# Regrouping the rows of a store-bound top-2 gate kernel: 65 and 63 rows to 64 and 64, and fewer first loads

## The chip, the cores and the metric

The kernel runs on one core of one Trainium2 chip. The metric is the device time of the program in microseconds; for the kernel before it is the median of three runs. A profile of one execution gives a span, the time from the first to the last instruction that the profiler recorded, which is about 2 us shorter than the device time.

## The reference: what is computed

There are 16 x 1024 = 16384 tokens. Each has a row of 512 float32 values in `x` and 8 router logits. The two largest of the 8 softmax probabilities, scaled so that they add up to 1, each multiply the token's row, and both products are written, the smaller weight first.

```python
probs = np.exp(router_logits - logits_max)
probs = probs / np.sum(probs, axis=-1, keepdims=True)
topk_indices = np.argsort(probs, axis=-1)[..., -k:]            # k = 2
topk_probs = np.take_along_axis(probs, topk_indices, axis=-1)
topk_probs = topk_probs / np.sum(topk_probs, axis=-1, keepdims=True)
x_expanded = x[:, :, np.newaxis, :].repeat(k, axis=2)
return (x_expanded * topk_probs[..., np.newaxis]).astype(np.float32)
```

So 33.5 MB of `x` and 0.5 MB of logits are read, and 67.1 MB are written. After the scaling the two weights depend only on the difference of the two largest logits, and the kernel computes them as two sigmoids of it.

## The kernel before

The 16384 tokens are 128 per partition. They are worked on in two groups, of 65 and 63 tokens ("rows") per partition. In a group, partition p holds consecutive tokens, so a load of n rows reads n x 2 KB in one piece for each partition, and a store of n rows writes n x 4 KB in one piece.

The tile `xs` holds a whole group of `x`; `osp` is an output buffer of 16 rows. Half of the output doesn't go through `osp`: a multiply writes its output over rows of `xs`, its own input among them. `over(r, n, G)` gives the place: twice the row number, less G, so that the output of the group's last rows ends with the group's last row.

```python
GROUPS = [65, 63]
LOADS = [[2, 2, 4, 8, 17, 28, 4], [16, 16, 31]]
LAST = [[(48, 9), (57, 8)], [(48, 15)]]

...  # the top-2 weights: 11 small VectorE operations and 2 ScalarE sigmoids, giving WA

    L = 16
    logits = wpool.tile([P, M, E], F32)
    xs = wpool.tile([P, max(GROUPS), D], F32)
    osp = wpool.tile([P, L, 2, D], F32)

    def over(r, n, G):
        a = 2 * r - G
        return xs[:, a : a + 2 * n, :].rearrange("p (r k) d -> p r k d", k=2)

    h = L // 2
    e = 2
    m0 = 0
    for g, G in enumerate(GROUPS):
        r = 0
        for n in LOADS[g]:
            nc.sync.dma_start(xs[:, r : r + n, :], x_v[g][:, r : r + n, :])
            r += n
            if g == 0 and r == L:
                nc.sync.dma_start(logits[:, :G], rl_v[0])
                nc.sync.dma_start(logits[:, G:], rl_v[1])
                WA = top2_weights(nc, wpool, logits, M, E)
        assert r == G
        begin = [(0, e, osp[:, :e]), (e, L - e, osp[:, e:])] if g == 0 else [(0, L, osp)]
        plan = begin + [
            (L, L, over(L, L, 2 * L)),      # output over xs[0:32]
            (2 * L, h, osp[:, :h]),
            (2 * L + h, h, osp[:, h:]),
        ]
        plan += [(r, n, over(r, n, G)) for r, n in LAST[g]]
        for r, n, og in plan:
            nc.vector.tensor_tensor(og, ...xs rows r to r + n, WA..., op=ALU.mult)
            queue = nc.scalar if n == e else nc.sync
            queue.dma_start(o_v[g][:, r : r + n], og)
        m0 += G
```

The stores of group 0 therefore have 2, 14, 16, 8, 8, 9 and 8 rows, those of group 1 have 16, 16, 8, 8 and 15. All loads and all stores but one are issued in this order from one queue, SyncE's. What a transfer or a multiply must wait for (a load before the multiply that reads it, a store before the rows it reads are overwritten) the framework puts in.

Of the kernel before, what the change touches and what calls it, by code (L numbers as in the profile page):

```python
# [1 line left out]

# [4 lines left out]

F32 = mybir.dt.float32
ALU = mybir.AluOpType
ACTF = mybir.ActivationFunctionType  # L10
P = 128


def top2_weights(nc, pool, logits, M, E):

    hi, lo, n = None, None, E  # L20
    while n > 1:
        n //= 2
        if hi is None:
            a, b = logits[:, :, 0:n], logits[:, :, n : 2 * n]
            nhi = pool.tile([P, M, n], F32, tag=f"hi{n}")
            nlo = b
            nc.vector.tensor_tensor(nhi, a, b, op=ALU.max)  # L27
            nc.vector.tensor_tensor(nlo, a, b, op=ALU.min)  # L28
        else:
            a, b = hi[:, :, 0:n], hi[:, :, n : 2 * n]  # L30
            nhi = pool.tile([P, M, n], F32, tag=f"hi{n}")
            nlo = pool.tile([P, M, n], F32, tag=f"lo{n}")
            tmp = pool.tile([P, M, n], F32, tag=f"tmp{n}")
            nc.vector.tensor_tensor(tmp, lo[:, :, 0:n], lo[:, :, n : 2 * n], op=ALU.max)  # L34
            nc.vector.tensor_tensor(nlo, a, b, op=ALU.min)  # L35
            nc.vector.tensor_tensor(nlo, nlo, tmp, op=ALU.max)  # L36
            nc.vector.tensor_tensor(nhi, a, b, op=ALU.max)  # L37
        hi, lo = nhi, nlo
    dlt = pool.tile([P, M], F32, tag="dlt")
    nc.vector.tensor_tensor(dlt, hi[:, :, 0], lo[:, :, 0], op=ALU.subtract)  # L40
    WA = pool.tile([P, M, 2], F32, tag="WA")
    nc.scalar.activation(WA[:, :, 0], dlt, ACTF.Sigmoid, scale=-1.0)  # L42
    nc.scalar.activation(WA[:, :, 1], dlt, ACTF.Sigmoid, scale=1.0)  # L43
    return WA

GROUPS = [65, 63]

LOADS = [[2, 2, 4, 8, 17, 28, 4], [16, 16, 31]]


LAST = [[(48, 9), (57, 8)], [(48, 15)]]


@with_exitstack
def kernel(
    ctx: ExitStack,
    tc: tile.TileContext,  # L60
    x: bass.AP,
    router_logits: bass.AP,
    k: bass.AP,
    out: bass.AP,
):
    nc = tc.nc
    B, S, D = x.shape
    E = router_logits.shape[-1]
    N = B * S
    assert int(k) == 2 and E == 8 and N == P * sum(GROUPS)  # L70
    M = N // P

    L = 16
    x_v, o_v, rl_v = [], [], []
    t0 = 0
    for n in GROUPS:
        t1 = t0 + P * n
        x_v.append(
            x.rearrange("b s d -> (b s) d")[t0:t1].rearrange("(p m) d -> p m d", p=P)
        )  # L80
        o_v.append(
            out.rearrange("b s k d -> (b s) k d")[t0:t1].rearrange(
                "(p m) k d -> p m k d", p=P
            )
        )
        rl_v.append(
            router_logits.rearrange("b s e -> (b s) e")[t0:t1].rearrange(
                "(p m) e -> p m e", p=P
            )
        )  # L90
        t0 = t1

    wpool = ctx.enter_context(tc.tile_pool(name="wpool", bufs=1))
# [28 lines that stand above are left out]
            (L, L, over(L, L, 2 * L)),  # L122
            (2 * L, h, osp[:, :h]),
            (2 * L + h, h, osp[:, h:]),
        ]
        plan += [(r, n, over(r, n, G)) for r, n in LAST[g]]
        for r, n, og in plan:
            nc.vector.tensor_tensor(  # L128
                og,
                xs[:, r : r + n, :].unsqueeze(2).to_broadcast([P, n, 2, D]),  # L130
                WA[:, m0 + r : m0 + r + n, :].unsqueeze(3).to_broadcast([P, n, 2, D]),
                op=ALU.mult,
# [7 lines that stand above are left out]
# [1 line left out]
_INS = ['x', 'router_logits', 'k']  # L141
_OUTS = [((16, 1024, 2, 512), 'float32')]

_NUMBERS = {'k': 2}


# [26 lines left out]
```

## Time and profile before

| | |
|---|---|
| time, median of 3 runs | 240.35 us (240.12 to 240.47) |
| span of the profiled execution | 238.4 us |
| VectorE busy | 142.0 us in 23 instructions, 138.2 of it in the 12 multiplies of line 128 |
| ScalarE busy | 1.8 us in 3 instructions |
| read from HBM, written to it | 34.08 MB, 67.11 MB |
| mean rate over the span | 424 GB/s |
| DMA issues | 10 loads of x, 2 of logits, 12 stores |

How to read it: the page cuts the span into 40 slices (6 us each) and prints the busy share of each engine in tenths; the row "DMA" is the mean of the core's 16 DMA engines. A packet is the piece that one DMA engine moves for one partition; "landing" is the moment at which a transfer has told its semaphore that all of it has arrived, so the time from issue to landing contains the time in the queue. The chain of waits follows the work that ended last back from the end. A group's line gives the operation, its shape, how often it ran, its busy time and mean duration, and after the bar the idle time of the engine before it and what ended most of that.

### The profile page before, as it was taken

How to read it: one execution, taken by the hardware profiler on the slowest of the kernel's cores; microseconds unless marked ns; L12 is line 12 of the kernel's file. 1: busy time of each engine (PE TensorE's matmuls, PEld its weight loads, DVE VectorE, ACT ScalarE, POOL GpSimd, SP SyncE). 2: the span in 40 equal slices, each digit the busy share in tenths (PEclk: the TensorE clock that was granted, in tenths of full speed). 3: DMA queues.
4: the chain of work that ended last, by engine and by line, in shares of the span. 5: the costliest groups of instructions: out<-in, count | busy, mean ns of one | idle time of the engine just before them, and what ended most of it. 6: DMA issues, size and time to landing. Idle time of an engine off the chain costs nothing.

```text
span 238.4 us, 118 instructions
## 1 busy us (share of the span) xinstructions
DVE 142.0 (60%) x23; ACT 1.8 (1%) x3; POOL 0.2 (0%) x4
## 2 busy tenths in 40 slices
DVE  0058999990299699900000699999006999990000
ACT  2000000000000000000000000000000000000000
POOL 0000000000000000000000000000000000000000
DMA  7999989999898999999999999999998989999995
GB/s 247 443 470 389 496 359 521 352 462 462 352 506 352 440 440 440 440 408 472 440 434 418 418 484 426 426 440 429 407 473 352 528 352 440 440 440 429 495 402 258
DMA packets 3456, 101.19 MB, mean 425 GB/s; under 512 B 384, under 2 KB 512, under 8 KB 896
## 3 DMA queue, kind: packets, MB, share of 16 engines
q1 hardware_dynamic: 3312, 100.14, 97.9%
q10 hardware_dynamic: 144, 1.05, 1.0%
HBM read 34.08 MB, written 67.11 MB: 424 GB/s over the span
## 4 chain that ended last, share of the span: by engine, by line
DMA 43%; DVE 41%; issue 5%; SPq 1%; ACT 0%; DVEq 0%
DVE xs L128 22%; DVE osp L128 17%; DMA xs<-in_x_dram 13%; DMA out_dram<-osp 13%; DMA out_dram<-xs 12%; DMA logits<-in_router_logits_dram 5%; SPq L112 1%; DVE nhi L27 0%; DVE logits L28 0%; SPq L116 0%; DVE nlo L36 0%; DVE tmp L34 0%; DVE nhi L37 0%; DVE nlo L35 0%; SPq L136 0%
## 5 line engine op out<-in xcount | busy, mean ns | idle before, releaser
L128 DVE TENSOR_TENSOR osp<-xs,WA 128x8192 f32<-128x8192 f32 (+3 forms) x7 | 69.1, 9908 | 55.5 <-DMA xs<-in_x_dram 31.1
L128 DVE TENSOR_TENSOR xs<-xs,WA 128x16384 f32<-128x16384 f32 (+3 forms) x5 | 69.1, 13811 | 2.2 <-DMA out_dram<-xs 2.1
L27 DVE TENSOR_TENSOR nhi<-logits 128x512 f32<-128x512 f32 x1 | 0.7, 693 | 14.6 <-DMA logits<-in_router_logits_dram 14.6
L42 ACT ACT_TABLE_LOAD x1 | 1.3, 1283 | 0.7 <-PEq L154 0.7
L28 DVE TENSOR_TENSOR logits<-logits 128x512 f32<-128x512 f32 x1 | 0.7, 691 | 0.0
L36 DVE TENSOR_TENSOR nlo<-nlo,tmp 128x256 f32<-128x256 f32 (+1 forms) x2 | 0.7, 350 | 0.0
L37 DVE TENSOR_TENSOR nhi<-nhi 128x256 f32<-128x256 f32 (+1 forms) x2 | 0.7, 350 | 0.0
L35 DVE TENSOR_TENSOR nlo<-nhi 128x256 f32<-128x256 f32 (+1 forms) x2 | 0.7, 349 | 0.0
L42 ACT ACTIVATE WA<-dlt 128x128 f32<-128x128 f32 x1 | 0.3, 314 | 16.5 <-DVE dlt L40 16.5
L34 DVE TENSOR_TENSOR tmp<-logits 128x256 f32<-128x256 f32 x1 | 0.4, 417 | 0.0
L40 DVE TENSOR_TENSOR dlt<-nhi,nlo 128x128 f32<-128x128 f32 x1 | 0.3, 292 | 0.0
L43 ACT ACTIVATE WA<-dlt 128x128 f32<-128x128 f32 x1 | 0.3, 298 | 0.0
L34 DVE TENSOR_TENSOR tmp<-nlo 128x128 f32<-128x128 f32 x1 | 0.3, 284 | 0.0
L154 POOL MEMSET const-bfloat16-1.0<- 128x1 bf16 x1 | 0.1, 101 | 0.0
L154 POOL MEMSET const-uint8-127<- 128x1 uint8 x1 | 0.1, 101 | 0.0
L154 POOL MEMSET const-float32-0.0<- 128x1 f32 x1 | 0.1, 98 | 0.2 <-issue 0.2
L154 POOL MEMSET const-float32-1.0<- 128x1 f32 x1 | 0.1, 98 | 0.0
## 6 DMA issues: line engine op xcount, KB each, us to landing
out_dram<-osp SPq DMA_DIRECT2D x4, 4096.0 KB, 20.7
xs<-in_x_dram SPq DMA_DIRECT2D x2, 4096.0 KB, 29.9
xs<-in_x_dram SPq DMA_DIRECT2D x1, 7936.0 KB, 37.9
out_dram<-xs SPq DMA_DIRECT2D x1, 7680.0 KB, 23.2
xs<-in_x_dram SPq DMA_DIRECT2D x1, 7168.0 KB, 39.7
out_dram<-osp SPq DMA_DIRECT2D x1, 7168.0 KB, 27.5
out_dram<-xs SPq DMA_DIRECT2D x1, 4608.0 KB, 20.3
xs<-in_x_dram SPq DMA_DIRECT2D x1, 4352.0 KB, 21.2
```

Source lines behind the costliest of these rows:

```text
L27: nc.vector.tensor_tensor(nhi, a, b, op=ALU.max)
L28: nc.vector.tensor_tensor(nlo, a, b, op=ALU.min)
L34: nc.vector.tensor_tensor(tmp, lo[:, :, 0:n], lo[:, :, n : 2 * n], op=ALU.max)
L35: nc.vector.tensor_tensor(nlo, a, b, op=ALU.min)
L36: nc.vector.tensor_tensor(nlo, nlo, tmp, op=ALU.max)
L37: nc.vector.tensor_tensor(nhi, a, b, op=ALU.max)
L40: nc.vector.tensor_tensor(dlt, hi[:, :, 0], lo[:, :, 0], op=ALU.subtract)
L42: nc.scalar.activation(WA[:, :, 0], dlt, ACTF.Sigmoid, scale=-1.0)
L43: nc.scalar.activation(WA[:, :, 1], dlt, ACTF.Sigmoid, scale=1.0)
L112: nc.sync.dma_start(xs[:, r : r + n, :], x_v[g][:, r : r + n, :])
L128: nc.vector.tensor_tensor(og, xs[:, r : r + n, :].unsqueeze(2).to_broadcast([P, n, 2, D]), WA[:, m0 + r : m0 + r + n, :].unsqueeze(3).to_b ...
L154: nc = _bacc.Bacc("TRN2", target_bir_lowering=False, num_devices=1)
```

## The change

Both groups get 64 rows. The last multiply and store of each group take 16 rows (64 KB in one piece for each partition in the store) in place of 9 and 8 in group 0 and 15 in group 1; the list `LAST` goes. The 16 rows before the logits come in two loads, of 2 and 14 rows (4 and 28 KB), in place of 2, 2, 4 and 8, and the 17-row load (34 KB) becomes one of 16. It is meant to make the schedule regular and its transfers fewer and longer.

```diff
+GROUPS = [64, 64]
 
-GROUPS = [65, 63]
+LOADS = [[2, 14, 16, 28, 4], [16, 16, 32]]
 
-LOADS = [[2, 2, 4, 8, 17, 28, 4], [16, 16, 31]]
-
-
-LAST = [[(48, 9), (57, 8)], [(48, 15)]]
@@
             (L, L, over(L, L, 2 * L)),
             (2 * L, h, osp[:, :h]),
             (2 * L + h, h, osp[:, h:]),
+            (3 * L, L, over(3 * L, L, G)),
         ]
-        plan += [(r, n, over(r, n, G)) for r, n in LAST[g]]
```

With 64 rows the last output of a group lies over `xs[32:64]`. A partition's rows then begin every 128 KiB in `x` and every 256 KiB in the output, where they began every 130 and 260 KiB in group 0 and every 126 and 252 KiB in group 1.

## The prediction

> **What bounds the kernel now.** I read the 40-slice picture first, because a kernel that moves 101 MB and does one multiply per output element is a transfer kernel until shown otherwise.
>
> ```profile
> DVE  0058999990299699900000699999006999990000
> ...
> DMA  7999989999898999999999999999998989999995
> ...
> DMA packets 3456, 101.19 MB, mean 425 GB/s; under 512 B 384, under 2 KB 512, under 8 KB 896
> ...
> q1 hardware_dynamic: 3312, 100.14, 97.9%
> q10 hardware_dynamic: 144, 1.05, 1.0%
> ```
>
> The DMA row is 8 or 9 in every slice but the first and the last; VectorE has whole runs of zeros. The two queues add up to 98.9% of 16 engines' span. So what sets the end is the number of bytes, the rate of the 16 DMA engines, the time until the first byte and the time after the last. VectorE (142 us of 238.4) only has to hand over each store before the queue in front of it is empty.
>
> The chain of waits seems to say something else: it names VectorE for 39% of the span, in several places. It must be read with that picture:
>
> ```profile
> 150.18 30.59 DMA out_dram<-osp
> ...
> 180.87 0.10 DVE osp L128
> 180.96 8.51 issue
> 189.47 8.70 DVE osp L128
> 198.17 0.02 issue
> 198.19 16.16 DVE xs L128
> ```
>
> A 16-row store issued at 150.18 lands 30.6 us later although its data need about 19 us: the rest is queue. While VectorE makes the last three stores (180.87 to 214.35), the engines work off earlier ones. Whether that holds at the end is in the landing times (start of the issue, plus the us to landing in the table of DMA issues, asked in small windows). Group 1's stores land at 180.8 (150.18 + 30.6), 200.1 (167.44 + 32.7), 209.8 (189.6 + 20.2), 219.5 (198.2 + 21.3) and 237.6 (214.38 + 23.2). The gaps, 19.3, 9.7, 9.7 and 18.1 us, are for 8.39, 4.19, 4.19 and 7.86 MB: 432 to 434 GB/s each time, so no hole lies between them. The last store was issued 5.1 us before its predecessor landed: that is the slack of the tail.
>
> The VectorE waits, in the groups kept apart by shape, say which transfers gate it:
>
> ```profile
> L128 DVE TENSOR_TENSOR osp<-xs,WA 128x8192 f32<-128x8192 f32 x4 | 34.6, 8688 | 23.8 <-DMA out_dram<-osp 23.8
> L128 DVE TENSOR_TENSOR osp<-xs,WA 128x16384 f32<-128x16384 f32 x1 | 17.2, 17225 | 31.1 <-DMA xs<-in_x_dram 31.1
> L128 DVE TENSOR_TENSOR xs<-xs,WA 128x15360 f32<-128x15360 f32 x1 | 16.2, 16157 | 0.0
> L128 DVE TENSOR_TENSOR xs<-xs,WA 128x9216 f32<-128x9216 f32 x1 | 9.8, 9759 | 2.1 <-DMA out_dram<-xs 2.1
> L128 DVE TENSOR_TENSOR xs<-xs,WA 128x8192 f32<-128x8192 f32 x1 | 8.7, 8692 | 0.0
> ```
>
> To be seen: 8 output rows cost 8.69 us, 16 cost 17.22; and the 9-row multiply waits 2.1 us for a store out of xs. With 65 rows its output is xs[31:49], and xs[31] is still being read by the 16-row store out of xs[0:32].
>
> **What the skill says.** "DMA: Bandwidth & Descriptors", section "Where 436 GB/s comes from", gives 435.2 GB/s as the ceiling of the 16 ports. The trace agrees: 436 GB/s from 133 to 168 us, 432 to 434 between landings. The kernel stands at its ceiling, and only what isn't streaming can be saved. The section "Anatomy of one DMA" of that page gives about 2 us fixed per DMA; the trace shows it hidden, as 4.19 MB stores land 9.7 us apart. The table of "Latency and other measured facts" warns of large power-of-two row pitches: copies between HBM tensors ran at 207 GB/s at a pitch of 512 KiB and 164 at 2 MiB, against 214. No run here shows this: the pitches now are 260 and 252 KB for the output, 130 and 126 KB for x. The change makes them exactly 256 and 128 KiB.
>
> **The change, part by part.** The bytes stay (34.08 MB read, 67.11 written), and so does VectorE's work but for the cutting. The unit prices, from landings: 32 input rows or 16 output rows 19.3 us, so an input row 0.6 us and an output row 1.2 us.
>
> (a) *Fewer transfers.* Loads go from 10 to 8, stores from 12 to 11, with the two logits loads 24 to 21. In the trace's packet records (one packet for each partition's row, 8 per engine and transfer) a 64 KB packet takes 2.418 us and a 32 KB one 1.213: a cut costs 0.008 us in each of 8 packets, 0.06 us per transfer. Three fewer save 0.2 us.
>
> (b) *The first loads.* 4, 4, 8 and 16 KB rows become 4 and 28 KB. The packet records: 128 packets of 4 KB at a mean of 0.256 us (the first of all, with the start-up in it), then 0.159, then 8 KB at 0.309, 16 KB at 0.611. Times 8 packets per engine: 2.05 + 1.27 + 2.47 + 4.89 = 10.68 us for 16 rows. After: 2.05 for the first, and for 28 KB by the line through 16 and 32 KB (0.611 + 12/16 x 0.602 = 1.06) 8.50, together 10.55. Gain 0.13 us, already the better part of (a), not beside it. The logits queue behind the same bytes; they land at 14.5 now and would at about 14.4. The issues (0.4 us each) lie far ahead of the data either way. The loads of 28 and 4 rows no longer wait about 0.9 us for reused semaphores before issue, but 20 us of queue is ahead of them: nothing.
>
> (c) *Groups of 64.* One input row (0.6 us) and one output row (1.2 us) move from group 0 to group 1: the middle of the schedule comes earlier, the sum doesn't change.
>
> (d) *One 16-row store at the end of group 0.* Its output is xs[32:64], clear of xs[0:32], so the 2.1 us wait goes. The 14-row store lands at 63.9 now, at 63.2 with one input row less in front; two 8-row multiplies (17.3 us) end at 80.5, the 16-row one (17.2) at 97.8. Now the two stores are handed over at 93.1 and 101.8. The queue in front lasts until the second 8-row store, which lands at 102.9 now (81.6 + 21.3) and at about 102.2 then. A fresh DMA needs about 1.1 us from issue to its first packet (the first load: issued at 0.73, first packet at 1.8). So 97.8 + 1.1 = 98.9 against about 101.5, when the first engines run out: 2.5 us of slack where there were 7.5. It shrinks and costs nothing.
>
> (e) *Group 1's third load* waits for that store to land: at about 121.4 in place of 123.4. Two 16-row loads (19.4 us) are then in front of it, so no hole.
>
> (f) *The last store, 16 rows.* The first store of group 1 lands at 180.8 - 1.2 - 0.2 = 179.4; then 17.3 us for two 8-row multiplies and 17.2 for 16 rows in place of 16.2: issue at 214.0. Its predecessor lands at 219.5 - 1.4 = 218.1, its first engines are free at about 217.3, and the store is ready at 215.1: 2.2 us of slack, against 3.3 now. The last store itself takes 19.3 us rather than 18.1, beginning 1.2 us earlier: no difference.
>
> Sum: -0.2 us from (a) and (b), nothing from (c) to (f). Another -0.2 stands if the replaced 31-row load was slow by chance of its form: its 63,488-byte packets have a median of 2.342 us but a mean of 2.367, 0.025 x 8 = 0.2. From 240.35 that makes 239.95; with +0.15 as the mean of a row pitch effect (below), 240.1.
>
> **The rivals.** First, *a hole in the queue*: if the 16-row multiply of group 0 waited for the store out of xs[0:32] as the 9-row one does, it would start near 82.5, be stored at 99.7 and have its first packet at 100.8: still just in time. For the tail, slack of 2.2 us would have to be lost altogether. Were both wrong by 3 us, the cost would be 1 to 2 us. Against it speak the landing gaps.
>
> Second, *the row pitch*. At 256 KiB, half the smallest pitch of the page's table, my estimate from that table is a loss of 0 to 1.5% on the stores, which are 155 us (67.11 MB at 434 GB/s): 0 to 2.3 us. For it: exact powers of two in every load and store, 16 engines in step. Against it: the loss at 512 KiB is only 3%, and the engines here are held by their own ceiling, so there may be room before HBM shows. With a loss as at 512 KiB on everything, the time would be near 248 (3.3% of 232 us).
>
> Third, *a gain at the start*: 16 rows at 434 GB/s need 9.7 us and take 10.7 now; if long rows brought all of that, 1.0 us is gained: 239.4. Against it: the first load with its start-up is unchanged.
>
> **Range and chances.** Predicted 240.1. Low end 239.4: the whole start gained. High end 241.2: a pitch loss of 0.7% on the stores, or one hole of 1 us. 2% is 4.8 us. Faster by that isn't possible: 101.19 MB at 435.2 GB/s are 232.5 us; with the first packet at 1.8 and 0.8 us from the last landing to the end, the span can't fall below 235.1, and the time is 2 us longer than the span (240.35 to 238.4). Slower by it needs 3% on the stores: 0.05.
>
> **What would show it.** Right: the DMA row stays at 8 and 9; landing gaps of 19.3 us for 16 output rows; no VectorE wait for a store out of xs; the last store of group 0 issued near 97.8, of group 1 near 214.0, each at least 2 us before its predecessor lands; the last landing near 237.3. Wrong: 64 KB packets that take more than 2.42 us or a mean rate under 423 GB/s (pitch); a landing gap longer than its bytes need, with the DMA row dipping near 100 or 216 us (hole); a first 16 rows that land over half a microsecond earlier (start).

## The result, and the profile after

The changed kernel takes 241.07 us (median of 6 runs, 240.95 to 241.82) against 240.26 us of the kernel before (6 runs, 240.12 to 240.47): a ratio of 1.0038, with a 95% interval of 1.0025 to 1.0052. It is 0.8 us slower. The predicted 240.1 us lay 0.16 us on the other side; the measured time lies within the range of 239.4 to 241.2, close to its upper end.

From the page of the kernel after: VectorE and DMA in 40 slices, the packets, and the two queues with their packets, MB and share of 16 engines' span.

```profile
span 239.2 us, 112 instructions
...
DVE  0058999990399999400000999998008999990000
...
DMA  7999898999989899999989998989999998999894
...
DMA packets 3024, 101.19 MB, mean 423 GB/s; under 512 B 336, under 2 KB 336, under 8 KB 720
...
q1 hardware_dynamic: 2880, 100.14, 97.6%
q10 hardware_dynamic: 144, 1.05, 1.0%
```

The same bytes in fewer packets, and no slice dips: no hole has opened that the slices would show, and yet the span is 0.8 us longer.

The end of the chain of waits after the change (start, duration, what):

```profile
149.05 31.15 DMA out_dram<-osp
...
180.23 0.04 DVE osp L125
180.26 8.57 issue
188.84 8.70 DVE osp L125
197.53 0.02 issue
197.55 17.22 DVE xs L125
```

It has the shape it had before. The last store follows at 214.81. Group 1's stores land at 180.2, 199.5, 209.2, 218.9 and 238.2, that is 19.3, 9.7, 9.7 and 19.3 us apart, each what its 8.39 or 4.19 MB need at 434 GB/s. The tail lost nothing, although its start is 0.8 us later than the predicted 179.4.

The multiplies by shape (busy us and mean ns, then the idle time before them and its cause):

```profile
L125 DVE TENSOR_TENSOR xs<-xs,WA 128x16384 f32<-128x16384 f32 x4 | 68.9, 17225 | 0.1
L125 DVE TENSOR_TENSOR osp<-xs,WA 128x8192 f32<-128x8192 f32 x4 | 34.6, 8688 | 24.1 <-DMA out_dram<-osp 24.1
...
L125 DVE TENSOR_TENSOR osp<-xs,WA 128x16384 f32<-128x16384 f32 x1 | 17.2, 17226 | 33.5 <-DMA xs<-in_x_dram 33.5
```

The wait for a store out of `xs` is gone, as foreseen: the four multiplies over `xs` stand idle for 0.1 us together.

The packet records (a start and a duration for each partition's row) show what the slices can't. I call *excess* what a packet takes beyond the shortest of its size, summed over a stretch and divided by the 16 engines (the packets of 4 bytes, one for each engine and transfer, are left out). Without any excess an engine's packets would take 233.85 us after the change and 234.04 before: the 0.19 us that the longer transfers were to save are there. The excess rose from 1.61 to 1.93 us. And the engines drifted apart: their last packets end within 1.04 us of each other, before within 0.48. In both kernels each engine moved 8 of the last store's 128 packets, so the slowest one sets the end: the mean end moved by 0.35 us, the last by 0.6. Net of the saving, then, only 0.13 us of the span's 0.83 is longer packets. Of the rest, 0.17 us is idle time of the engines in the first 14 us, 0.25 the wider spread of their ends, and 0.22 lies behind the last packet (1.14 us before, 1.36 after), where the 65-row grid below, which loses next to nothing, has 1.36 too.

### The profile page after: what moved, and what is told of

Same layout as the page of the kernel before. It is cut to its first block, busy times and chain, and to the rows that moved or that the text cites. A ratio compares the mean times of both kernels' runs of the same rounds, so it can differ in the third digit from the quotient of the medians.

```text
span 239.2 us, 112 instructions
## 1 busy us (share of the span) xinstructions
DVE 141.8 (59%) x22; ACT 1.8 (1%) x3; POOL 0.2 (0%) x4
## 4 chain that ended last, share of the span: by engine, by line
DMA 43%; DVE 38%; issue 7%; SPq 1%; ACT 0%; DVEq 0%
DMA out_dram<-osp 24%; DVE osp L125 22%; DVE xs L125 14%; DMA xs<-in_x_dram 14%; DMA logits<-in_router_logits_dram 5%; SPq L109 0%; DVE nhi L27 0%; DVE logits L28 0%; DVE nlo L36 0%; DVE nlo L35 0%; DVE tmp L34 0%; DVE nhi L37 0%; SPq L113 0%; SPq L133 0%; ACT WA L42 0%
## 5 line engine op out<-in xcount | busy, mean ns | idle before, releaser
L125 DVE TENSOR_TENSOR xs<-xs,WA 128x16384 f32<-128x16384 f32 x4 | 68.9, 17225 | 0.1
```

What stands on the lines that cost most here:

```text
L125: nc.vector.tensor_tensor(og, xs[:, r : r + n, :].unsqueeze(2).to_broadcast([P, n, 2, D]), WA[:, m0 + r : m0 + r + n, :].unsqueeze(3).to_b ...
```

## The experiments

### Which part of the change costs: first loads or groups

Two kernels take the change apart. Only the first loads, in the kernel before:

```diff
-LOADS = [[2, 2, 4, 8, 17, 28, 4], [16, 16, 31]]
+LOADS = [[2, 14, 17, 28, 4], [16, 16, 31]]
```

> The kernel before with only its first loads changed: 2 and 14 rows in place of 2, 2, 4 and 8; groups of 65 and 63 and all stores as before. Theory A (the regrouping costs: equal groups with power-of-two row pitches, and the 16-row stores at the end of both groups): no loss here, 240.1 us, 0.1 under before for two transfers less. Theory B (the first loads cost: with fewer and longer first transfers the 16 DMA engines start and end less evenly; in the changed kernel the last packets of the engines end over 1.04 us, before over 0.48): the whole loss, 240.9 to 241.1 us, with the wide end spread.

Measured: 240.51 us (21 runs) against 240.37, ratio 1.0007 (1.0001 to 1.0014). The first loads bring no gain; they cost about 0.17 us. The engines end within 0.52 us of each other, so theory B falls in both of its parts.

Only the regrouping, in the changed kernel:

```diff
-LOADS = [[2, 14, 16, 28, 4], [16, 16, 32]]
+LOADS = [[2, 2, 4, 8, 16, 28, 4], [16, 16, 32]]
```

> The changed kernel with the old first loads (2, 2, 4, 8, then 16, 28, 4): only the regrouping and the 16-row last stores are left. Theory A (regrouping costs): 240.9 to 241.1 us. Theory B (first loads cost): 240.1 to 240.3 us, end spread of the engines about 0.5 us. If both parts cost a share, this run and the other one add up to 0.8 us.

Measured: 241.56 us (240.85 to 242.87), ratio 1.0048 (1.0029 to 1.0067). The loss sits with the groups. The profiled execution was the longest of the six, and in it the engines drifted furthest apart, as the page's slices and the first queue's share show:

```profile
span 241.1 us, 115 instructions
...
DMA  6999898998999999999899999898989899999891
...
q1 hardware_dynamic: 3168, 100.14, 96.9%
```

The last slice is busy for a tenth where the kernel before has five: in the packet records 15 engines are done by 237.5 us, and one works alone until 239.9. The mean end, 237.4, is 0.1 us from that of the changed kernel. The gap opened in steps: the engines' signals of one landing were 1.3 us apart at 14 us already, and 3.0 at 163 us.

### Is it the small packets at the hand-over from loads to stores

Around 44 us, where the first loads end and the stores take over, the 8 KB packets of group 0's last load are slow. Two kernels have no such load.

```diff
-LOADS = [[2, 14, 16, 28, 4], [16, 16, 32]]
+LOADS = [[2, 14, 16, 32], [16, 16, 32]]
```

> The changed kernel with group 0's last two loads (28 and 4 rows) as one of 32. In both traces the 8 KB packets of the 4-row load, the last before the stores take over, are slow: mean 0.371 us before and 0.420 after, where 0.309 is usual; times 8 packets per engine 0.5 and 0.9 us. Theory C (the hand-over from loads to stores costs by the packet, small ones most): this gets back 0.5 to 0.8 us of it, 240.3 to 240.5 us. If the hand-over costs the same time whatever packet is there (the slow time moves into the last 64 KB packets): 241.0 us, nothing gained.

```diff
-LOADS = [[2, 2, 4, 8, 17, 28, 4], [16, 16, 31]]
+LOADS = [[2, 2, 4, 8, 17, 32], [16, 16, 31]]
```

> The kernel before with 28 and 4 rows as one load of 32. Theory C (small packets at the hand-over cost): 239.8 to 240.0 us, 0.3 to 0.5 us under before. If the hand-over costs the same whatever the packet: 240.2 us.

Measured: 241.26 us, ratio 1.0041 (1.0029 to 1.0053), and 240.39 us, ratio 1.0001 (0.9994 to 1.0009). Nothing was gained by either. In the second, the excess of the 8 KB packets fell from 0.50 to 0.02 us, and that of the 64 KB packets rose from nothing to 0.58; in the first, 0.92 us in 8 KB packets became 1.01 in 64 KB ones. In each kernel the hand-over costs about the same whatever packet it meets; theory C falls.

### Stores or row pitch

The regrouping does two things: it makes the last stores longer and hands them over later, and it sets the rows of the partitions exactly 128 KiB apart in `x` and 256 KiB in the output. Three kernels change one of these with all else kept, and the changed kernel runs beside them.

The first has the changed kernel's transfers, but takes them from a grid of 65 rows to a partition:

```diff
-    for n in GROUPS:
-        t1 = t0 + P * n
+    for g, n in enumerate(GROUPS):
+        w = n + 1
+        t0 = g * (N - P * w)
+        t1 = t0 + P * w
...  # x, output and logits seen as [P, w] rows from t0 to t1; the 65th row is not touched
```

> The changed kernel, all transfers and multiplies of the same sizes in the same order, but with both groups' rows of a partition 130 KiB apart in x and 260 KiB in the output, as group 0 had them before; the 65th row of each partition and group is left out and 512 rows are done twice, so the output is not complete. Theory P (the power-of-two pitch of the equal groups costs): the loss goes, 240.1 to 240.4 us, and the 16 DMA engines end within about 0.5 us of each other. Theory S (the order and size of the stores cost, the 16-row last ones with the third load's wait for one of them): 241.0 us, as the changed kernel.

The rows done twice are 249, and as many are left out.

The second splits the last stores:

```diff
-            (3 * L, L, over(3 * L, L, G)),
+            (3 * L, h, over(3 * L, h, G)),
+            (3 * L + h, h, over(3 * L + h, h, G)),
```

> The changed kernel with the last 16 rows of each group in two multiplies and stores of 8 rows (32 KB a row) in place of one of 16: the old way of handing over early, at the new pitch. Theory S (the 16-row last stores cost): 240.2 to 240.5 us. Theory P (pitch): 241.0 us or 0.1 more for two further transfers.

The third doubles the pitch:

```diff
-            x.rearrange("b s d -> (b s) d")[t0:t1].rearrange("(p m) d -> p m d", p=P)
+            x.rearrange("b s d -> (b s) d").rearrange("(p m) d -> p m d", p=P)[:, m0:m1]
...  # the same for the output and the logits; m0 and m1 bound the group's rows
```

> The changed kernel with each partition's 128 rows in one piece, so that the pitch is doubled: 256 KiB in x and 512 KiB in the output, for both groups; all sizes and the order are the same, the output complete. Theory P (power-of-two pitch): the loss grows, 242 us or more (twice the loss, 241.9, to the 3 per cent of the skill's table at 512 KiB, 248), and wider ends of the engines. Theory S: 241.0 us, no difference.

> The changed kernel unaltered, on the chip of the three above, as their yardstick: 241.0 to 241.3 us by every theory, the engines' ends about 1 us apart.

Measured: off the powers of two 240.54 us, ratio 1.0007 (0.9998 to 1.0017); doubled 242.63 us, ratio 1.0096 (1.0080 to 1.0111); the changed kernel again 241.26 us, ratio 1.0033 (1.0015 to 1.0051). With the same transfers at another pitch nearly all of the loss is gone, and at the doubled pitch it is larger; theory P stands. The doubled pitch costs 2.2 us and so lands within what was expected, though far from the 3 per cent of the table that the prediction cites. That it is the power of two which counts, and not any multiple of 128 KiB, is not shown: 384 KiB, for one, was not tried. With split stores the time is 240.98 us, ratio 1.0022 (1.0015 to 1.0030): most of the loss remains, and as the interval overlaps that of the unsplit kernel, whether splitting gives back a share is not settled. The spread of the engines' ends does not go with the loss: 0.74 us on the grid (0.5 had been expected), 0.94 at the doubled pitch, which was to be the widest, 1.26 in the changed kernel again, and 0.67 with split stores, less than the 0.77 of the kernel before with a 32-row load, which loses nothing.

Where the time goes is seen between two events: the issue of group 0's last store and the start of group 1's first multiply, which waits for the load behind that store. The lines are from the order of time; start, duration, what, and in brackets the wait. First the grid of 65 rows (130 and 260 KiB), then the doubled pitch (256 and 512 KiB):

```profile
98.00 0.33 SPq L133 DMA_DIRECT2D out_dram<-xs  x1
...
131.34 17.23 DVE L125 TENSOR_TENSOR osp<-xs,WA 128x16384 f32<-128x16384 f32 x1 [33.37 <-DMA xs<-in_x_dram]
```

```profile
97.85 0.33 SPq L133 DMA_DIRECT2D out_dram<-xs  x1
...
132.60 17.23 DVE L125 TENSOR_TENSOR osp<-xs,WA 128x16384 f32<-128x16384 f32 x1 [34.78 <-DMA xs<-in_x_dram]
```

The store is issued 0.15 us earlier at the doubled pitch, the multiply starts 1.26 later: 1.41 us go in 33, over the turn from stores to loads. In the packet records it is the last packets of the store and the first ones of the load that are slow: those started from 117 to 124 us have an excess of 1.32 us per engine, at 130 and 260 KiB 0.06. A smaller part lies at the turn back from loads to stores, from 155 to 162 us: 0.51 us, on the grid 0.21. From 14 to 40 us, where loads run (from 25 us on with the 2-row store's packets between them), and from 162 to 240, where only stores run, the excess stays under 0.05 us at either pitch; there a 64 KB store packet takes 2.418 us as ever. All told the excess grew by 1.82 us, and the span by 1.83 (238.85 to 240.68).

### The pitch of the loads or of the stores

The doubled pitch split in two, and the same for the change's own pitch. The first kernel has the doubled pitch in `x` with the 65-row grid in the output:

```diff
     x_v.append(x...rearrange("(p m) d -> p m d", p=P)[:, m0 : m0 + n])
-    o_v.append(out...rearrange("(p m) k d -> p m k d", p=P)[:, m0 : m0 + n])
+    o_v.append(out...[t0:t1].rearrange("(p m) k d -> p m k d", p=P))
```

> The doubled pitch (242.63 us) split in two. Here x keeps its pitch of 256 KiB, but the output's is 260 KiB, as in group 0 of the kernel before; sizes and order are the changed kernel's. The rows go to other places of the output and some are written twice, so the output is not the reference's. Theory W (the stores' pitch costs): 240.5 us, as with both pitches off powers of two. Theory R (the loads' pitch costs, as it is load packets that are slow in the traces): 242.6 us.

The second has it the other way round:

```diff
-    x_v.append(x...rearrange("(p m) d -> p m d", p=P)[:, m0 : m0 + n])
+    x_v.append(x...[t0:t1].rearrange("(p m) d -> p m d", p=P))
     o_v.append(out...rearrange("(p m) k d -> p m k d", p=P)[:, m0 : m0 + n])
```

> The other half: x at 130 KiB, the output at 512 KiB; one row of each 65 of x is left out and some are loaded twice, so the output is not the reference's. Theory W (the stores' pitch costs, by making loads slow that run beside them): 242.6 us. Theory R (the loads' pitch): 240.5 us. If both are in between, near 241.5, each has a share or only their meeting counts.

The third starts from the 65-row grid and gives the output back the change's own groups of 64:

```diff
-            out.rearrange("b s k d -> (b s) k d")[t0:t1].rearrange(
+            out.rearrange("b s k d -> (b s) k d")[
+                g * P * n : (g + 1) * P * n
+            ].rearrange(
```

> The changed kernel with only x moved back to a pitch of 130 KiB; the output keeps the change's 256 KiB. One row of each 65 of x and of the logits is left out and some are loaded twice, so the output is not the reference's. With both pitches off powers of two the time was 240.54, with both on them (the changed kernel) 241.07 and 241.26. If the output's pitch makes the loss at this size too: 240.9 to 241.2 us. If it is x's: 240.4 to 240.6 us. In between: each has a share.

All pitch kernels together. The sixth column is the time from the issue of group 0's last store to group 1's first multiply, the seventh the excess of the packets started from 117 to 124 us, both in us of one profiled execution. The times come from several chips; each ratio is to the kernel before on the same chip, so the ratios are what to compare.

| x, KiB | output, KiB | time, us | ratio to before | 95% interval | store to multiply | excess at the turn |
|---|---|---|---|---|---|---|
| 130 | 260 | 240.54 | 1.0007 | 0.9998 to 1.0017 | 33.34 | 0.06 |
| 256 | 260 | 240.98 | 1.0037 | 1.0023 to 1.0051 | 33.58 | 0.11 |
| 128 | 256 (the change) | 241.07 | 1.0038 | 1.0025 to 1.0052 | 33.44 | 0.13 |
| 128 | 256 (again) | 241.26 | 1.0033 | 1.0015 to 1.0051 | 33.53 | 0.33 |
| 130 | 256 | 241.11 | 1.0033 | 1.0021 to 1.0045 | 33.78 | 0.42 |
| 130 | 512 | 242.63 | 1.0097 | 1.0084 to 1.0110 | 34.67 | 1.08 |
| 256 | 512 | 242.63 | 1.0096 | 1.0080 to 1.0111 | 34.75 | 1.32 |

With `x` off the powers of two the loss of 512 KiB and that of 256 KiB are there in full, so the output's pitch is enough to make the change's loss, as theory W has it. But `x` is not free, which theory W did not expect: 256 KiB in `x` alone costs as much (1.0037) as 256 KiB in the output alone (1.0033), though the turn hardly shows it (0.11 us), and next to the output's 512 KiB it adds nothing. In these seven rows the ratio follows the larger power-of-two pitch, whichever side has it: 1.0007 with none, 1.0033 to 1.0038 at 256 KiB, 1.0096 and 1.0097 at 512. Why the two sides do not add up is open. Whether `x` at the change's 128 KiB costs by itself was not tried; beside the output's 256 KiB it adds nothing that shows. These are the two timelines that differ in the output's pitch alone, 512 KiB and then the 256 KiB of the change, both with `x` at 130:

```profile
98.27 0.33 SPq L129 DMA_DIRECT2D out_dram<-xs  x1
...
132.94 17.22 DVE L121 TENSOR_TENSOR osp<-xs,WA 128x16384 f32<-128x16384 f32 x1 [34.69 <-DMA xs<-in_x_dram]
```

```profile
97.97 0.33 SPq L135 DMA_DIRECT2D out_dram<-xs  x1
...
131.75 17.23 DVE L127 TENSOR_TENSOR osp<-xs,WA 128x16384 f32<-128x16384 f32 x1 [33.81 <-DMA xs<-in_x_dram]
```

Against the grid's 131.34, the multiply starts 0.41 us later at 256 KiB, after a store issued at the same time within 0.03; the span is 0.37 longer (239.22 against 238.85). So with `x` kept at 130, the whole difference of these two executions arises at the turn. In the changed kernel itself it is spread otherwise. In both its profiles group 0's last multiply begins 0.3 to 0.4 us later than on the grid (81.10 and 81.19 against 80.75), before any turn from stores to loads, behind engines that are further apart. This lag does not follow the pitch: at 256 and 512 KiB the multiply begins at 80.60. As single executions of a kernel differ by a few tenths, I take the size of its loss from the timed runs and not from these pieces.

### What a late hand-over costs

The prediction said that the slack before the end of the queue covers the later hand-over. To see such a slack overdrawn, the last 17 rows of group 0 in the kernel before go in one multiply and store:

```diff
-LAST = [[(48, 9), (57, 8)], [(48, 15)]]
+LAST = [[(48, 17)], [(48, 15)]]
```

> The kernel before, groups of 65 and 63, with the last 17 rows of group 0 in one multiply and store in place of 9 and 8. This multiply has to wait for the store out of the first 32 rows of xs (83.3 us in the profile of before) and takes 18.3 us, so the store is handed over at 101.6 and its first packet can start at about 102.7, when the engines run out of work between 101.8 and 102.3: a hole of 0.4 to 0.9 us. If such a hole in the queue is what a late hand-over costs: 240.7 to 241.2 us, with the DMA engines idle near 102 us. If the queue covers it: 240.3 us.

Measured: 242.88 us, ratio 1.0114 (1.0101 to 1.0127): 2.6 us, where 0.5 to 1.0 was expected. Its timeline, and then that of the kernel before:

```profile
83.99 18.29 DVE L128 TENSOR_TENSOR xs<-xs,WA 128x17408 f32<-128x17408 f32 x1 [2.11 <-DMA out_dram<-xs]
102.31 0.39 SPq L136 DMA_DIRECT2D out_dram<-xs  x1
...
135.20 17.22 DVE L128 TENSOR_TENSOR osp<-xs,WA 128x16384 f32<-128x16384 f32 x1 [32.92 <-DMA xs<-in_x_dram]
```

```profile
101.82 0.33 SPq L136 DMA_DIRECT2D out_dram<-xs  x1
...
132.93 17.23 DVE L128 TENSOR_TENSOR osp<-xs,WA 128x16384 f32<-128x16384 f32 x1 [31.14 <-DMA xs<-in_x_dram]
```

The hole is there, and a little over the expected 0.4 to 0.9 us. In the packet records the engines end the store in front between 101.9 and 102.8 us and all start the new one at 103.2 to 103.4: 1 us of idleness. The rest is excess: 0.78 us per engine from 117 to 124 us (0.003 in the kernel before) and 1.02 in the last load before 162 us (0.19 before). That the hole caused this, by setting all engines to the same beat, is a guess and not shown; a 68 KB row is also moved as two packets of 34 KB, so this kernel differs in more than the hole.

## Why the prediction was right, and where it was wrong

The prediction forecast a gain of 0.25 us, 240.35 to 240.1, and a loss of 0.8 came. The measured time lies within its range because the upper end allowed for the rival that came true, a pitch loss. That it stays 0.13 us inside, although the savings failed too, is luck.

**What bounds the kernel**: right. The DMA row stays full. At the doubled pitch the loss is time in which the engines move the same bytes for longer (1.82 us of excess for 1.83 of span, against the grid). In the changed kernel's profile that is a small part, and the rest is at the start, in the engines' ends and behind the last packet.

**(a), (b), the transfers saved**: the saving was right by its own term and wrong in what it brought. Packet time without excess fell by 0.19 us as worked out. But the kernel with the first loads alone is 0.02 to 0.34 us slower, not 0.13 faster: its time without excess fell by 0.26 us, and its excess at the hand-over near 44 us rose from 0.49 to 0.91, with the start's falling from 0.82 to 0.59. The full change without its pitch is at 1.0007, where (a), (b) and the second 0.2 us made 0.9983. The 0.2 us for the 31-row load was mistaken too: the 32-row load has the same excess (0.17 us from 155 to 162 us, 0.19 before), and the kernel with the first loads alone, which keeps the 31-row load, has 0.01. So it is not the load's form.

**(c), (d), (e), the middle**: right in kind. The 2.1 us wait is gone. The store was handed over at 98.36 us, 97.8 predicted, without a hole; the third load waits until 122.1, 121.4 predicted. Each came 0.5 to 0.7 us late, because of the 0.7 us by which this part was to run ahead, 0.6 were lost on the way to 64 us: the 14-row store landed at 63.8, not at 63.2. One landing was misread, with little effect: the second 8-row store was issued at 81.3 before, not at 81.6, and landed at 102.6, not at 102.9.

**(f), the tail**: right. The last store was issued at 214.81 (214.0 predicted), 4.1 us before its predecessor landed, as 218.1 less 214.0 had said.

**The rivals**: the hole did not come in the changed kernel, and the run with 17 rows shows that the slack was real, and dear to overdraw. The gain at the start did not come: 16 rows land at 13.2 us in both kernels. The row pitch is what happened.

**The step that failed** is the sum. Its last term, "+0.15 as the mean of a row pitch effect", measured 0.6 to 0.75 us: the changed kernel at 1.0033 and 1.0038 against 1.0007 for the same transfers on the 65-row grid, and on the same chip 241.26 against 240.54. The mechanism had been named, within 0 to 2.3 us; its mean was set too low. The savings of 0.4 us did not come at all. With the pitch term as measured and no savings, the sum would have been 240.95 to 241.1.

One sign in the list of signs was wrong as well. Pitch was to show in 64 KB packets of more than 2.42 us or a mean rate under 423 GB/s. Where stores run alone the packets stayed at 2.418, at 512 KiB too, and the changed kernel's rate was 423, not under it (at the doubled pitch it was 420). In the whole execution 81 of 768 packets of 64 KB took over 2.42 us, but so did 54 of 768 on the grid, which loses next to nothing. The sign could not have told the true cause at the change's pitch.

The Trainium skill's table in "DMA: Bandwidth & Descriptors", section "Latency and other measured facts", has a loss of 3% at 512 KiB, for copies between HBM tensors. This kernel loses 1.0% there. Why it is less here was not tested. The excess sits mostly at the turns between loads and stores, but that both run side by side is not enough for it: at 512 KiB, too, the 128 packets of the 2-row store, which went out among the loads from 25 to 43 us, took 0.309 us each, as on the grid.

None of the kernels tried is faster than the kernel before; the nearest are its variant with a 32-row load at 1.0001, and the one with fewer first loads and the 65-row grid, both at 1.0007.

## What to carry to other kernels

In a kernel bound by transfers, choose the rows per partition with the pitch in HBM in mind: with all sizes equal, rows 130 and 260 KiB apart beat rows 128 and 256 KiB apart. In the change the output's pitch, twice the input's, was enough for the loss; at an equal 256 KiB either side alone cost about the same. Look for such a loss in the packets at the turns between loads and stores, not in the rate of a steady stretch, and trust the timed runs for its size, as single profiles differ by as much. And do not count on a saving of a few tenths from fewer transfers: the 0.2 us less of packet time was there, and the kernel was no faster.

## What the runs showed of the hardware

- A row pitch of 256 KiB, in the output or in the input alone, cost 0.6 to 0.7 us of 240, and 512 KiB in the output 2.1 to 2.2. At 512 KiB 1.1 to 1.3 us of excess lay in packets started from 117 to 124 us, at the turn from stores to loads, and under 0.05 us each in those from 14 to 40 us and from 162 us on.
- The first turn from loads to stores (40 to 46 us) had 0.33 to 1.01 us of excess for each engine in the 14 profiles, and about the same in 8 KB packets as in 64 KB ones (0.50 and 0.58 in the kernel before).
- The engines share no work of a transfer: in one execution an engine began its last packet at 237.5 us, when another had been done since 237.1, and the program waited for it until 239.9.
- A hole of 1 us in the queue came with a loss of 2.6 us.
